# A two-layer encoder: the FFN in four rounds, its raw weights in activation buffers, its scale at the output sums

## The chip, the cores and the metric

The kernel runs on one core of a Trainium2 chip. The metric is the device time of one execution in microseconds, the median of several runs. The engines are TensorE (PE, matrix products into PSUM), VectorE (DVE), ScalarE (ACT), GpSimd (POOL), and SyncE (SP), whose queue starts most of the DMA transfers; GpSimd starts those that add to what lies at their target. Each engine takes its instructions in order.

## The reference

Two layers, each on x of 512 positions by 1024 channels, all in float32. The first part of a layer mixes attention, a convolution and a Fourier transform and ends in an output projection and a residual add. The change is in the second part, the FFN with D_FF = 2816:

```python
x = x + merged @ w_out[l]

h2 = rmsnorm(x, norm2_g[l])
f_gate, f_up = jnp.split(h2 @ w_ffn_in[l], 2, axis=-1)
x = x + (jax.nn.silu(f_gate) * f_up) @ w_ffn_out[l]
```

## The kernel before

Everything is held with channels on the 128 partitions and the 512 positions along a row; x is eight tiles of 128 x 512 (`x2[m]`). A float32 product is made of three matmuls at reduced precision: each operand is split into a high part (a copy to fp32r) and a low part (operand minus high part), and high x high, high x low and low x high are summed in PSUM. So every weight and every activation has two buffers.

Weights come in chunks of 128 x 1024 (512 KB), each loaded by SyncE into a `raw` buffer. `WB` gives the numbers of buffers for raw, high and low chunks: 3, 3 and 5. `chunk` (L192) prepares an ordinary chunk: a ScalarE copy gives the high part (L203), and a VectorE subtraction the low part (L205). In the FFN (`by_dma`, `low_by_dma` L275) the low part is made otherwise: ScalarE writes the negated raw weight, rounded, into the low buffer (L276), and a DMA started by GpSimd adds the weight from HBM to it (L277).

The FFN's hidden channels are 22 tiles of 128. One tile is a unit: a gate tile and an up tile, two sums over eight tiles of x. A unit is computed by the scheme of Strassen and Winograd with seven products instead of eight. `combine` (L296) makes the combinations of x once per layer (`us`, `ts`, in buffers of `at`, `X` and `B`); `pair_weights` (L232) makes those of the weights from two raw chunks (quarters a11, a12, a21, a22), with sums s1, s2, s4 on VectorE (L259, L263, L267), a difference written over a21 in the raw buffer (L260), high copies (L261, L266), and low parts (L262 for half of `l1`, by DMA for the other half and for `l2`). The sums' splits take buffers of `att` for the first four units of a layer, else of `A`. `pair_gemm` (L316) runs four products of 256 columns, copies and adds them to `p15` (L335, L336), then runs three more. Its two PSUM banks are of tag `s`, `att` or `main` in turn, by the unit's number modulo 3; `main` has three banks, the others two.

`unit` (L526) then scales gate and up by `rb2`, the inverse RMS of each position (L529 to L536), with Silu on ScalarE (L532), multiplies them (L537) and splits the result into buffers of `wth`, `wtl`, `qst`/`kst` or `att`. After eleven units, `gemm` makes eight output sums over these eleven tiles in `main` banks, and L556 adds each to `x2[m]`. The second half does the same with the other eleven; there x goes to HBM or, in layer 0, also to the next layer's first split (`next_x`, with L158 on VectorE and an addition L360 on GpSimd).

Before the FFN, the output projection runs over the split tiles `ms`, which lie in `cv` and `A`. For each of its sums the residual is loaded (L513), added (L517), scaled (L518) and combined.

The order of instructions on each engine is set by a planner that simulates the program; each piece has a due time (`self.at`). Weights of a unit are due `WLS` = 26000 ns before their use, ordinary chunks `WL` = 16000.

Of the kernel before, what the change touches and what calls it, by code (L numbers as in the profile page):

```python
# [9 lines left out]
F32 = mybir.dt.float32  # L10
# [3 lines left out]
ALU = mybir.AluOpType  # L14
AX = mybir.AxisListType

P = 128
# [43 lines left out]
WB = (3, 3, 5)  # L61
WLS = 26000
HALF = 108
PASS = 216
# [24 lines left out]
class Hybrid:  # L89
# [102 lines left out]
    def chunk(self, l, c, t):  # L192
# [8 lines left out]
        if self.by_dma:  # L201
            self.low_by_dma(lo, raw, self.a["w"][l, c])
        nc.scalar.copy(hi, raw)  # L203
        if not self.by_dma:
            nc.vector.tensor_tensor(out=lo, in0=raw, in1=hi.bitcast(F32), op=ALU.subtract)  # L205
# [26 lines left out]
    def pair_weights(self, early):  # L232
# [3 lines left out]
        raws = []  # L236
        for _ in range(2):
            raw = self.wp.tile([P, CHUNK * P], F32, tag="raw", name=self.nm("wr"), bufs=WB[0])
            c, k = divmod(self.wi, CHUNK)
            assert k == 0  # L240
            nc.sync.dma_start(raw, self.a["w"][self.l, c])
            self.wi += CHUNK
            raws.append(raw)
        r1, r2 = raws
        a21, a11 = r1[:, 0:T], r1[:, T : 2 * T]
        a22, a12 = r2[:, 0:T], r2[:, T : 2 * T]
        tags = ("qst", "kst", "ar") if early else ("cv", "cv", "cv")
        s1, s2, s4 = (self.slot(tag) for tag in tags)
        out = {}

# [4 lines left out]
        c = self.wi // CHUNK - 2  # L255
        self.low_by_dma(l1[:, T : 2 * T], a11, self.a["w"][self.l, c][:, T : 2 * T])
        self.low_by_dma(l2, r2, self.a["w"][self.l, c + 1])
        g = nc.vector.tensor_tensor
        g(out=s1, in0=a21, in1=a22, op=ALU.add)  # L259
        g(out=a21, in0=a11, in1=a21, op=ALU.subtract)  # L260
        nc.scalar.copy(h1, r1)  # L261
        g(out=l1[:, 0:T], in0=a21, in1=h1[:, 0:T].bitcast(F32), op=ALU.subtract)  # L262
        g(out=s2, in0=s1, in1=a11, op=ALU.subtract)  # L263
        for name, src in (("s1", s1), ("s2", s2)):
            out[name] = self.split_to(src, "att" if early else "A")
        nc.scalar.copy(h2, r2)  # L266
        g(out=s4, in0=a12, in1=s2, op=ALU.subtract)  # L267
        out["s4"] = self.split_to(s4, "att" if early else "A")
# [5 lines left out]

    def low_by_dma(self, lo, raw, src):  # L275
        self.nc.scalar.activation(lo, raw, AF.Copy, scale=-1.0)  # L276
        self.nc.gpsimd.dma_start(lo, src, accum_op=ALU.add)  # L277
# [193 lines left out]
    def main(self, l):  # L471
# [7 lines left out]
        self.by_dma = False  # L479
# [46 lines left out]
        def unit(j, b1, b2, qw):  # L526
# [9 lines left out]
            v(out=u, in0=u, in1=rb2, op=ALU.mult)  # L536
# [4 lines left out]
            if j < 7:  # L541
                return self.split_to(u, "qst", "kst")
            return self.split_to(u, "att")

        self.by_dma = True
        for half in range(2):
            act = []
            for j in range(NJ // 2):
                w = self.pair_weights(half == 0 and j < 4)
                got = self.pair_gemm(j, w, xc, half == 0 and j == 0)  # L550
                if half == 0 and j == 0:
                    rb2 = self.inv_rms(acc, D, "M", "rb")
                act.append(unit(j, *got))
            for m in range(KT):
                ps = self.gemm(act)
                nc.vector.tensor_tensor(out=x2[m], in0=ps, in1=x2[m], op=ALU.add)  # L556
                if half == 0:
                    continue
# [512 lines left out]
def _pack(inp, l):  # L1071
# [3 lines left out]
    def add(w):  # L1075
        seq.append(_tiles(w).reshape(-1, P, P))
# [35 lines left out]
    for half in range(2):  # L1112
        for j in range(half * NJ // 2, (half + 1) * NJ // 2):
            for k in range(2):
                for o in (FF, 0):
                    add(w1[k * D // 2 : (k + 1) * D // 2, o + j * P : o + (j + 1) * P])
        add(w2[half * FF // 2 : (half + 1) * FF // 2])
# [80 lines left out]
```

## Time and profile before

| what | value |
|---|---|
| median of 3 runs | 1646.55 us (1642.36 to 1651.85) |
| the profiled execution, its own time | 1652.3 us |
| its span in the profile | 1650.5 us |
| mean granted clock of TensorE | 0.99 |
| TensorE busy | 1601.2 us, 97% of the span |
| VectorE busy | 1247.5 us, 76% |
| ScalarE busy | 889.0 us, 54% |
| GpSimd busy | 229.3 us, 14% |
| moved by DMA | 236.47 MB |

In the profile a busy time is what an engine spent in instructions; for TensorE it includes pipelining, so a busy engine is not always one at its peak. A wait is put down to the instruction that ended it. The chain of waits follows the work that ended last back from the end, at each step to what released it. PEclk is the granted share of TensorE's full clock. In the views, a line number such as L262 is that of the kernel before, `wr` is a raw chunk, `wh`/`wl` are high and low parts of an ordinary chunk, `whi`/`wlo` of a unit's.

### The profile page before, as it was taken

How to read it: one execution, taken by the hardware profiler on the slowest of the kernel's cores; microseconds unless marked ns; L12 is line 12 of the kernel's file. 1: busy time of each engine (PE TensorE's matmuls, PEld its weight loads, DVE VectorE, ACT ScalarE, POOL GpSimd, SP SyncE). 2: the span in 40 equal slices, each digit the busy share in tenths (PEclk: the TensorE clock that was granted, in tenths of full speed). 3: DMA queues.
4: the chain of work that ended last, by engine and by line, in shares of the span. 5: the costliest groups of instructions: out<-in, count | busy, mean ns of one | idle time of the engine just before them, and what ended most of it. 6: DMA issues, size and time to landing. Idle time of an engine off the chain costs nothing.

```text
span 1650.5 us, 24460 instructions
## 1 busy us (share of the span) xinstructions
PE 1601.2 (97%) x9096; PEld 1397.1 (85%) x9096; DVE 1247.5 (76%) x2308; ACT 889.0 (54%) x1399; POOL 229.3 (14%) x217
## 2 busy tenths in 40 slices
PE   8999999999999999999999999998999899999999
PEld 6888888887889888999888888886878798889887
DVE  7899999897878833885269999997877887257840
ACT  6345555773566644666443455457535665545651
POOL 4000000113321111112200000000142111111110
PEclk8999999999999999999999999999999899999999
DMA  5545233322467797778743642332225667976784
GB/s 191 172 139 159 77 109 106 104 75 83 132 158 169 158 216 182 166 168 211 201 131 90 190 126 84 107 105 71 84 87 150 148 156 173 211 168 165 178 210 122
DMA packets 80471, 236.47 MB, mean 143 GB/s; under 512 B 11088, under 2 KB 11984, under 8 KB 80352
## 3 DMA queue, kind: packets, MB, share of 16 engines
q1 hardware_dynamic: 60912, 176.11, 33.4%
q0 software_dynamic: 19440, 58.81, 21.2%
q8 instruction: 71, 1.16, 0.3%
q14 instruction: 48, 0.39, 0.1%
HBM read 220.98 MB, written 13.89 MB: 142 GB/s over the span
## 4 chain that ended last, share of the span: by engine, by line
PE 72%; DMA 11%; DVE 11%; ACT 3%; issue 2%; SPq 0%; DVEq 0%; ACTq 0%
PE main L121 53%; DMA wr<-in_w 11%; PE s L121 4%; PE att L121 3%; PE oth L121 3%; PE att L288 3%; PE s L288 3%; PE att L131 2%; PE main L288 1%; DVE wr L260 1%; DVE cv L259 1%; DVE wlo L262 1%; DVE A L155 1%; DVE cv L263 1%; DVE cv L267 1%
## 5 line engine op out<-in xcount | busy, mean ns | idle before, releaser
L203 ACT CAST wh<-wr 128x1024 fp32r<-128x1024 f32 x180 | 188.5, 1049 | 210.7 <-PE main L121 103.4
L121 PE MATMUL main<-X,wh 128*128 128x512 f32 x864 | 278.3, 396 | 0.0
L205 DVE TENSOR_TENSOR wl<-wr,wh 128x1024 fp32r<-128x1024 f32 x136 | 178.6, 1313 | 28.9 <-ACT wh L203 28.0
L121 PEld LDWEIGHTS main<-X,wh 128*128 128x128 f32 x864 | 161.8, 189 | 32.6 <-issue 0.5
L997 DVE SCALAR_TENSOR_TENSOR cv<-cv,hcw,cv 128x497 f32<-128x497 f32 (+14 forms) x240 | 176.5, 735 | 1.3
L121 PE MATMUL main<-X,wl 128*128 128x512 f32 x432 | 170.3, 394 | 0.0
L276 ACT ACTIVATE wlo<-wr 128x512 fp32r<-128x512 f32 x88 | 74.0, 844 | 125.5 <-DMA wr<-in_w 120.4
L277 POOL DMA_DIRECT2D wlo<-in_w x88 | 76.5, 869 | 413.6 <-ACT wlo L276 286.5
L121 PE MATMUL main<-att,wh 128*128 128x512 f32 x384 | 119.6, 391 | 3.0 <-ACT att L154 3.0
L821 ACT ACTIVATE at<-s,mx 128x512 f32<-128x512 f32 x128 | 87.9, 688 | 62.2 <-DVE mx L819 58.3
L556 DVE TENSOR_TENSOR V<-main,V 128x512 f32<-128x512 f32 x32 | 22.1, 691 | 126.3 <-PE main L121 126.2
L121 PE MATMUL main<-A,wh 128*128 128x512 f32 x320 | 105.9, 391 | 0.0
L121 PE MATMUL main<-wh,X 128*128 128x512 f32 x288 | 96.5, 391 | 0.0
L121 PEld LDWEIGHTS main<-X,wl 128*128 128x128 f32 x432 | 81.7, 189 | 16.8 <-issue 0.2
L819 DVE TENSOR_REDUCE mx<-s 128x1 f32<-128x512 f32 x128 | 86.6, 681 | 5.1 <-PE s L121 4.6
L276 ACT ACTIVATE wl<-wr 128x1024 fp32r<-128x1024 f32 x44 | 46.6, 1059 | 80.5 <-DMA wr<-in_w 78.7
L121 PEld LDWEIGHTS main<-att,wh 128*128 128x128 f32 x384 | 71.7, 188 | 19.0 <-ACT att L154 3.5
L259 DVE TENSOR_TENSOR cv<-wr,wr 128x512 f32<-128x512 f32 x36 | 25.0, 693 | 82.3 <-DMA wr<-in_w 82.3
L121 PE MATMUL main<-cv,wh 128*128 128x512 f32 x240 | 78.1, 394 | 4.9 <-ACT cv L154 4.8
L121 PE MATMUL main<-act,wh 128*128 128x512 f32 x256 | 80.6, 394 | 0.2 <-ACT wh L203 0.2
L1028 POOL TENSOR_TENSOR cv<-cv,cv 128x512 f32<-128x512 f32 x6 | 9.0, 1492 | 510.1 <-DVE cv L997 449.8
L155 DVE TENSOR_TENSOR A<-cv,A 128x512 fp32r<-128x512 f32 x108 | 73.7, 684 | 3.6 <-ACT A L154 3.6
(329 smaller groups left out, 4326.9 us busy)
## 6 DMA issues: line engine op xcount, KB each, us to landing
wr<-in_w SPq DMA_DIRECT2D x268, 512.0 KB, 4.4
wlo<-in_w POOLq DMA_DIRECT2D x44, 512.0 KB, 5.6
wl<-in_w POOLq DMA_DIRECT2D x44, 512.0 KB, 7.3
wlo<-in_w POOLq DMA_DIRECT2D x44, 256.0 KB, 4.5
dqk<-at SPq DMA_DIRECT2D x32, 256.0 KB, 3.7
qst<-dqk SPq DMA_DIRECT2D x96, 64.0 KB, 1.9
kst<-dqk SPq DMA_DIRECT2D x96, 64.0 KB, 2.0
V<-in_xT SPq DMA_DIRECT2D x8, 256.0 KB, 7.5
```

What stands on the lines that cost most here:

```text
L121: return self.pin(self.nc.tensor.matmul(out, lhsT=lhsT, rhs=rhs, start=start, stop=stop))
L131: self.pin(self.nc.tensor.transpose(ps[:, s], src[:, s], self.ident))
L155: nc.vector.tensor_tensor(out=lo, in0=src, in1=hi.bitcast(F32), op=ALU.subtract)
L203: nc.scalar.copy(hi, raw)
L205: nc.vector.tensor_tensor(out=lo, in0=raw, in1=hi.bitcast(F32), op=ALU.subtract)
L259: g(out=s1, in0=a21, in1=a22, op=ALU.add)
L276: self.nc.scalar.activation(lo, raw, AF.Copy, scale=-1.0)
L277: self.nc.gpsimd.dma_start(lo, src, accum_op=ALU.add)
L288: self.nc.tensor.matmul(ps, lhsT=a[:, s], rhs=b, start=start and k == ks[0] and i == 0, stop=last and i == 2, skip_group_check=True,)
L819: nc.vector.tensor_reduce(out=mx, in_=ps, axis=AX.X, op=ALU.max, negate=True)
L821: nc.scalar.activation(e, ps, AF.Exp, bias=mx, accum_out=z1 if c else z0)
L997: ins = nc.vector.scalar_tensor_tensor(out=acc[:, a:b], in0=g[:, a + d : b + d], scalar=w[:, t : t + 1], in1=acc[:, a:b], op0=ALU.mult, op ...
```

## The change

The FFN runs in four rounds of 6, 6, 6 and 4 units instead of two of 11, each followed by eight output sums over its tiles. Raw weights of odd units go into four half buffers of 128 x 512, of `att` for unit 1 and of `cv` for the others; those of even units stay in `raw`. The first sums s1 and s2 lie in `ar` (unit 0), `att` (unit 1) or `cv`, s4 takes the place of s1, and the splits of the sums go to `A` for odd units and to `qst`/`kst` for even ones. High buffers become four and low ones four. The low part `l1` is now wholly a VectorE subtraction; `l2` is still made by the DMA. Chunks of the output weights are split like all others, by a VectorE subtraction. The product of the up branch with `rb2` is left out of `unit`; instead each output sum is multiplied by `rb2` into a buffer of `M` and then added to `x2[m]`. The weights are packed on the host in the new order.

```diff
--- before.py
+++ after.py
@@ -58,9 +58,10 @@
 PEORD = False
 CONV_LOW = -20000
 WL = 16000
-WB = (3, 3, 5)
+WB = (3, 4, 4)
 WLS = 26000
 HALF = 108
+ROUNDS = (6, 6, 6, 4)
 PASS = 216
 MAGIC = 0x5F3759DF
 
@@ -198,11 +199,8 @@
         nc.sync.dma_start(raw, self.a["w"][l, c])
         hi = self.wp.tile([P, CHUNK * P], F32R, tag="hi", name=self.nm("wh"), bufs=WB[1])
         lo = self.wp.tile([P, CHUNK * P], F32R, tag="lo", name=self.nm("wl"), bufs=WB[2])
-        if self.by_dma:
-            self.low_by_dma(lo, raw, self.a["w"][l, c])
         nc.scalar.copy(hi, raw)
-        if not self.by_dma:
-            nc.vector.tensor_tensor(out=lo, in0=raw, in1=hi.bitcast(F32), op=ALU.subtract)
+        nc.vector.tensor_tensor(out=lo, in0=raw, in1=hi.bitcast(F32), op=ALU.subtract)
         tc.cur_priority = keep
         return hi, lo
 
@@ -229,52 +227,65 @@
         self.at(self.t)
         return ps
 
-    def pair_weights(self, early):
+    def pair_raw(self, u):
+        nc = self.nc
+        c, k = divmod(self.wi, CHUNK)
+        assert k == 0
+        self.wi += 2 * CHUNK
+        out = []
+        for i in range(2):
+            src = self.a["w"][self.l, c + i]
+            if u % 2 == 0:
+                raw = self.wp.tile([P, CHUNK * P], F32, tag="raw", name=self.nm("wr"), bufs=WB[0])
+                nc.sync.dma_start(raw, src)
+                out.append((raw[:, 0:T], raw[:, T : 2 * T], raw))
+            else:
+                halves = []
+                for o in (0, T):
+                    half = self.slot("att" if u == 1 else "cv")
+                    nc.sync.dma_start(half, src[:, o : o + T])
+                    halves.append(half)
+                out.append((*halves, None))
+        return out, self.a["w"][self.l, c + 1]
+
+    def pair_weights(self, u):
         nc, tc = self.nc, self.tc
         keep = tc.cur_priority
         self.at(self.t - WLS)
-        raws = []
-        for _ in range(2):
-            raw = self.wp.tile([P, CHUNK * P], F32, tag="raw", name=self.nm("wr"), bufs=WB[0])
-            c, k = divmod(self.wi, CHUNK)
-            assert k == 0
-            nc.sync.dma_start(raw, self.a["w"][self.l, c])
-            self.wi += CHUNK
-            raws.append(raw)
-        r1, r2 = raws
-        a21, a11 = r1[:, 0:T], r1[:, T : 2 * T]
-        a22, a12 = r2[:, 0:T], r2[:, T : 2 * T]
-        tags = ("qst", "kst", "ar") if early else ("cv", "cv", "cv")
-        s1, s2, s4 = (self.slot(tag) for tag in tags)
+        ((a21, a11, r1), (a22, a12, r2)), src2 = self.pair_raw(u)
+        s1, s2 = (self.slot(("ar", "att")[u] if u < 2 else "cv") for _ in range(2))
+        tags = ("A", "A") if u % 2 else ("qst", "kst")
         out = {}
-
         h1, l1, h2, l2 = (
             self.wp.tile([P, CHUNK * P], F32R, tag=tag, name=self.nm("w" + tag), bufs=WB[i])
             for tag, i in (("hi", 1), ("lo", 2), ("hi", 1), ("lo", 2))
         )
-        c = self.wi // CHUNK - 2
-        self.low_by_dma(l1[:, T : 2 * T], a11, self.a["w"][self.l, c][:, T : 2 * T])
-        self.low_by_dma(l2, r2, self.a["w"][self.l, c + 1])
         g = nc.vector.tensor_tensor
+
+        def parts(raw, a, b):
+            return ((slice(0, T), a), (slice(T, 2 * T), b)) if raw is None else ((slice(0, 2 * T), raw),)
+
+        for o, x in parts(r2, a22, a12):
+            nc.scalar.activation(l2[:, o], x, AF.Copy, scale=-1.0)
+        nc.gpsimd.dma_start(l2, src2, accum_op=ALU.add)
         g(out=s1, in0=a21, in1=a22, op=ALU.add)
         g(out=a21, in0=a11, in1=a21, op=ALU.subtract)
-        nc.scalar.copy(h1, r1)
-        g(out=l1[:, 0:T], in0=a21, in1=h1[:, 0:T].bitcast(F32), op=ALU.subtract)
-        g(out=s2, in0=s1, in1=a11, op=ALU.subtract)
-        for name, src in (("s1", s1), ("s2", s2)):
-            out[name] = self.split_to(src, "att" if early else "A")
-        nc.scalar.copy(h2, r2)
-        g(out=s4, in0=a12, in1=s2, op=ALU.subtract)
-        out["s4"] = self.split_to(s4, "att" if early else "A")
+        g(out=s2, in0=a22, in1=a21, op=ALU.subtract)
+        for o, x in parts(r1, a21, a11):
+            nc.scalar.copy(h1[:, o], x)
+        out["s1"] = self.split_to(s1, *tags)
+        for o, x in parts(r1, a21, a11):
+            g(out=l1[:, o], in0=x, in1=h1[:, o].bitcast(F32), op=ALU.subtract)
+        out["s2"] = self.split_to(s2, *tags)
+        for o, x in parts(r2, a22, a12):
+            nc.scalar.copy(h2[:, o], x)
+        g(out=s1, in0=a12, in1=s2, op=ALU.subtract)
+        out["s4"] = self.split_to(s1, *tags)
         for names, hi, lo in ((("s3", "a11"), h1, l1), (("a22", "a12"), h2, l2)):
             for i, n in enumerate(names):
                 out[n] = (hi[:, i * T : (i + 1) * T], lo[:, i * T : (i + 1) * T])
         tc.cur_priority = keep
         return out
-
-    def low_by_dma(self, lo, raw, src):
-        self.nc.scalar.activation(lo, raw, AF.Copy, scale=-1.0)
-        self.nc.gpsimd.dma_start(lo, src, accum_op=ALU.add)
 
     def product(self, ps, w, xs, ks, start, stop):
         wh, wl = w
@@ -476,7 +487,6 @@
         hcw = sm(4 * CW, "hcw")
         nc.vector.tensor_scalar_mul(hcw, self.par(l, "cw"), 0.5)
         self.hb, self.hcw = hb, hcw
-        self.by_dma = False
         self.glu(l)
         if l == 0:
             self.tables()
@@ -533,28 +543,28 @@
             u = self.slot("M")
             v(out=u[:, 0:h], in0=b2[:, h:T], in1=qw[:, 0:h], op=ALU.add)
             v(out=u[:, h:T], in0=qw[:, 0:h], in1=qw[:, h:T], op=ALU.add)
-            v(out=u, in0=u, in1=rb2, op=ALU.mult)
             v(out=u, in0=u, in1=z, op=ALU.mult)
             if j < 4:
                 t = self.wtp.tile([P, 2, T], F32R, tag="wth" if j < 2 else "wtl", name=self.nm("act"))
                 return self.split(u, t[:, 0, :], t[:, 1, :])
-            if j < 7:
-                return self.split_to(u, "qst", "kst")
             return self.split_to(u, "att")
 
-        self.by_dma = True
-        for half in range(2):
+        done = 0
+        for rnd, nj in enumerate(ROUNDS):
             act = []
-            for j in range(NJ // 2):
-                w = self.pair_weights(half == 0 and j < 4)
-                got = self.pair_gemm(j, w, xc, half == 0 and j == 0)
-                if half == 0 and j == 0:
+            for j in range(nj):
+                w = self.pair_weights(done + j)
+                got = self.pair_gemm(done + j, w, xc, done + j == 0)
+                if done + j == 0:
                     rb2 = self.inv_rms(acc, D, "M", "rb")
                 act.append(unit(j, *got))
+            done += nj
             for m in range(KT):
                 ps = self.gemm(act)
-                nc.vector.tensor_tensor(out=x2[m], in0=ps, in1=x2[m], op=ALU.add)
-                if half == 0:
+                y = self.slot("M")
+                nc.vector.tensor_tensor(out=y, in0=ps, in1=rb2, op=ALU.mult)
+                nc.vector.tensor_tensor(out=x2[m], in0=y, in1=x2[m], op=ALU.add)
+                if done < NJ:
                     continue
                 if l == L - 1:
                     nc.sync.dma_start(self.out[m], x2[m])
...
```

## Rows read from the trace of the kernel before

**Rows 1.** windows, halves of both FFNs: stretch, us, engines busy (count), clock, DMA share
```profile
462.50:649.50 187.00, 178.47 (x1191) 163.71 (x1191) 119.67 (x216) 107.04 (x149) 32.86 (x37) 0.98 0.76 176
649.50:825.70 176.20, 172.94 (x1190) 160.95 (x1190) 106.18 (x192) 100.21 (x139) 33.30 (x36) 1.00 0.76 186
1278.50:1469.20 190.70, 179.12 (x1191) 165.05 (x1190) 119.32 (x216) 106.82 (x148) 32.63 (x37) 0.97 0.75 173
1469.20:1646.90 177.70, 173.22 (x1190) 160.65 (x1188) 98.12 (x183) 90.14 (x122) 25.17 (x29) 1.00 0.72 169
```

**Rows 2.** chain that ended last (start us, us, what): TensorE pieces without stall
```profile
71.53 2.04 PE main L121 x9
...
752.29 4.32 PE s L288 x36
```

**Rows 3.** TensorE waits, whole span (us in total, times, longest): L288
```profile
PE s L288 <- ACT whi L261: 8.5, 7, 3.6
...
PE s L288 <- DVE at L155: 4.8, 2, 2.4
...
PE main L288 <- ACT M L335: 2.8, 5, 1.1
PE main L288 <- ACT whi L261: 2.2, 2, 1.3
...
PE att L288 <- ACT whi L261: 1.9, 3, 1.0
...
PE s L288 <- ACT M L335: 0.8, 2, 0.4
```

**Rows 4.** chain within 670 to 715 us: one turn of loading
```profile
677.79 4.45 DMA wr<-in_w
...
687.14 0.70 DVE wlo L262
...
687.85 4.46 DMA wr<-in_w
```

**Rows 5.** waits of SyncE's DMA queue, whole span: unit weights
```profile
SPq L241 <- DVE wlo L262: 257.6, 34, 11.7
```

**Rows 6.** windows: just after the stall at 470.9 us in layer 0
```profile
470.90:477.10 6.20, 6.16 (x24) 5.13 (x25) 4.99 (x8) 2.89 (x5) 1.28 (x1) 0.52 0.70 165
```

**Rows 7.** timeline of SyncE's queue before the first FFN
```profile
456.12 9.43 SPq L241 DMA_DIRECT2D wr<-in_w  x2
465.60 0.42 SPq L513 DMA_DIRECT2D M<-in_xT  x1
```

**Rows 8.** timeline of ScalarE before the first FFN
```profile
460.05 0.63 ACT L276 ACTIVATE wlo<-wr 128x512 fp32r<-128x512 f32 x1 [5.42 <-DMA wr<-in_w]
```

**Rows 9.** VectorE groups, 462.5 to 1647 us: busy, mean ns, idle before
```profile
L205 DVE TENSOR_TENSOR wl<-wr,wh 128x1024 fp32r<-128x1024 f32 x68 | 89.0, 1309 | 19.6 <-ACT wh L203 19.4
...
L259 DVE TENSOR_TENSOR cv<-wr,wr 128x512 f32<-128x512 f32 x36 | 25.0, 693 | 82.3 <-DMA wr<-in_w 82.3
...
L556 DVE TENSOR_TENSOR V<-main,V 128x512 f32<-128x512 f32 x32 | 22.1, 691 | 126.3 <-PE main L121 126.2
```

**Rows 10.** windows: unit stretches of layer 0's second half
```profile
650.00:760.00 110.00, 106.74 (x881) 105.77 (x880) 87.08 (x164) 68.57 (x100) 17.33 (x20) 1.00 0.73 171
680.00:700.00 20.00, 20.00 (x167) 19.84 (x166) 18.00 (x35) 13.49 (x21) 3.45 (x4) 1.00 0.73 176
```

**Rows 11.** timeline of VectorE at the first border from units to sums
```profile
597.85 0.69 DVE L537 TENSOR_TENSOR M<-M,M 128x512 f32<-128x512 f32 x1 [5.13 <-ACT M L532]
```

**Rows 12.** timeline of GpSimd, end of layer 0
```profile
820.25 1.30 POOL L360 TENSOR_TENSOR M<-M,M 128x512 f32<-128x512 f32 x1 [6.28 <-ACT M L357]
```

**Rows 13.** timeline of VectorE, the same stretch
```profile
815.64 1.23 DVE L205 TENSOR_TENSOR wl<-wr,wh 128x1024 fp32r<-128x1024 f32 x1 [2.83 <-ACT wh L203]
...
821.12 1.51 DVE L205 TENSOR_TENSOR wl<-wr,wh 128x1024 fp32r<-128x1024 f32 x1 [0.75 <-ACT wh L203]
...
827.75 0.75 DVE L158 SCALAR_TENSOR_TENSOR B<-V,par,A 128x512 fp32r<-128x512 f32 x1
```

More of the change, by code (lines that the diff above doesn't have):

```diff
@@ L1111, in _pack @@
     w1, w2 = inp["w_ffn_in"][l], inp["w_ffn_out"][l]
-    for half in range(2):
-        for j in range(half * NJ // 2, (half + 1) * NJ // 2):
+    done = 0
+    for nj in ROUNDS:
+        for j in range(done, done + nj):
             for k in range(2):
@@ L1116, in _pack @@
                     add(w1[k * D // 2 : (k + 1) * D // 2, o + j * P : o + (j + 1) * P])
-        add(w2[half * FF // 2 : (half + 1) * FF // 2])
+        add(w2[done * P : (done + nj) * P])
+        done += nj
     s = np.concatenate(seq, 0)
```

## The prediction

> **What bounds the kernel now.** TensorE is the engine that the rest feeds, so I read first, by windows, the two FFN stages, the only place where the order of work changes: four halves of 187.0, 176.2, 190.7 and 177.7 us [rows 1], 731.6 in all. Then the chain that ended last, for what these halves would take with TensorE never waiting: nine 512-column matmuls follow each other in 2.04 us, 0.2267 each, and 36 of 256 columns in 4.32, 0.120 each [rows 2]. A unit (one `pair_gemm`) has 7 products of 12 narrow matmuls, 84 x 0.120 = 10.08 us; eleven make 110.9. The eight output sums of a half are 8 x 11 x 3 = 264 wide ones, 59.8 us. A half without a stall is 170.7. The four lose 16.3, 5.5, 20.0 and 7.0, together 48.8 us. This is all that the change can win: it leaves every matmul as it was.
>
> Third, TensorE's own waits on L288, for what these 48.8 are. For high halves of weights (`whi`) 8.5 + 2.2 + 1.9 = 12.6 us; for evictions of a unit (L335, L336) 8.0 in five groups, of which the first and the last on L335 are shown; for the activations' combinations (`at`) at the stage's start 4.8, with two smaller groups 6.0 [rows 3]. With 0.7 of others that is 27.3. The other 21.5 are refill of the pipeline behind each wait and stretches at the lower clock: the 6.2 us after the stall at 470.9 ran at a granted 0.52, near the lower of the two levels (1.2 of 2.4 GHz) [rows 6], and cost about 3.
>
> Last, the chain inside a unit stretch, which says why weights are late. A raw load takes 4.45 us, its `raw` buffer is free only after VectorE's L262, the next load starts behind that, and the turn from load to load is 687.85 - 677.79 = 10.06 us here [rows 4], as long as the unit itself, with nothing to spare. SyncE's queue says the same: its unit loads waited 34 times, 257.6 us in all, for L262 [rows 5]. The longest stall, 3.6 us, is a first product waiting for its high half [rows 3].
>
> **The change part by part.** *Raw weights in two pools.* Even units keep the three `raw` buffers, odd ones take four half buffers of `att` or `cv`; each pool then turns once in two units, 20.2 us of TensorE for a turn of about 10 to 11 [rows 4]. High buffers go from 3 to 4 and splits alternate between `A` and `qst`/`kst`, so a unit's weights no longer wait for its neighbour's products. I take all 12.6 us of `whi` waits as gone, with their part of the 21.5 of refill and clock, 21.5 x 12.6 / 27.3 = 9.9: 22.5 together. Next to come late are the evictions; their 8.0 + 6.3 I leave as they are (bounds: all won, or as much again lost: -14.3 to +14.3).
>
> *The stage's start.* At 456.12 SyncE took 9.43 us over two raw loads for lack of a buffer, and the residual's load L513 stood behind them until 465.60 [rows 7]; ScalarE stood 5.42 us before a negation whose raw had not landed [rows 8], with the scaling L518 that the combination needs queued behind it. So `at` came late. Unit 1's raw now goes to `att` buffers that are long free, and neither queue should stand so long. Against that, the splits of unit 1 go to `A`, which the output projection holds to its last matmul: ScalarE's copy waits there, and its other work (L518, L357) behind it. The start's price is 6.0 + 21.5 x 6.0 / 27.3 = 10.7; I take half, 5.4 (0 to 10.7).
>
> *VectorE's load.* Per layer: 22 output chunks split by a subtraction, x 1.309 = 28.8 us; `l1` whole instead of half, 22 x (1.309 - 0.693) = 13.6; 64 evictions of output sums where 16 were, so 48 more at 0.69 = 33.1; the 22 products with `rb2` gone, -15.2 (same size as L259) [rows 9]. That is +60.3 a layer, 120.6 for both. VectorE had 443.3 us in the four halves [rows 1]; 563.9 in stages of some 713 is a share of 0.79. It reached 0.79 over 110 us of units, and 0.90 over 20 us in which TensorE never stopped [rows 10], though it stood 82.3 us behind raw loads at L259 alone [rows 9]. It fits, and I cost it at nothing while it is covered by output sums, which had VectorE mostly idle and now come after 4 or 6 units instead of 11; what it costs without that cover is a rival below. Halves of the loads double the issues of odd units on SyncE; only loads queue there, with the residual and the results at the stage's ends. GpSimd keeps one accumulating DMA a unit of two, and none for output chunks; ScalarE loses the negations. I count no gain for these: neither is what TensorE waits for.
>
> *More borders.* Units give way to sums at eight borders instead of four. A sum can run only up to the last unit's tile before that unit is evicted. At the border at 591 us that tile's product with the gate (L537) came at 597.85, held 5.13 us by ScalarE's Silu [rows 11]; no stall followed, since three `main` banks with ten tiles each gave 3 x 10 x 3 x 0.2267 = 20 us of other work. In the new rounds of 6 a bank gives 3 x 5 x 0.2267 = 3.4 us, and units 5, 11 and 17, which end the first three, hold two of the three `main` banks themselves (`u % 3` is 2) until they are evicted; in the round of 4 three free banks give 6.1. So the cover is 3.4 to 10.2 us for a chain that took about 8 here, and ScalarE no longer has negations of chunks in its queue. Bounds per border 0 to about 5 (8 less 3.4), 0 to 40 in all; I take 1 each, 8, nearer to the lower end since 10.2 covers the row seen.
>
> *The ends.* After the last matmul there is one VectorE instruction more, 0.69 [rows 9]. At layer 0's end the last round has 12 matmuls per sum, 2.72 us, against VectorE's two evictions, half a chunk and the next layer's split, 0.69 + 0.69 + 0.65 + 0.75 [rows 9, 13] = 2.78. I take 1 us (0 to 11, below).
>
> Sum: -22.5 - 5.4 + 8 + 0.7 + 1 = -18.2 us. Against the profiled execution (span 1650.5, its own time 1652.3) that is 1634. It lay 5.75 above the median of the three runs; the same sum from the median 1646.55 gives 1628.
>
> **The rivals.** *All of it goes.* If the evictions follow the weights too, and borders are free, 46 of the 48.8 are won: 1601. For it: 20 us at 680 ran without a stall [rows 10]. Against: eviction waits have nothing to do with the ring.
>
> *The ring was mostly hidden.* Then only the 12.6 and some 3 of lower clock come back, and the eviction waits double by 8, since weights that are ready early stand in VectorE's queue ahead of evictions: -7, 1639. For it: TensorE waits only 12.6 us by name for weights [rows 3] while the loads wait 257.6 [rows 5]. It is also what comes if the extra buffers don't lengthen the turn.
>
> *VectorE becomes the bound (slower).* 563.9 us of work in order, with each wait of the queue's head paid by all behind it. At share s the two stages take 563.9 / s: as long as now at 0.771, and slower by over 0.5% (8.2 us) below 0.762; at 0.75 it is 751.9, +20, 1667. Place: the last two units of a round, where chunk subtractions come on top of the units' own 17 instructions, and sums whose banks wait for an eviction. For it: the 0.79 over 110 us is near [rows 10]. Against: that share was held down by the loads that the change frees.
>
> *The layer's end collides.* A subtraction of 1024 columns that began while GpSimd's 1.30 us addition ran [rows 12] took 1.51 us where another took 1.23 [rows 13]. In the last round there is one such addition per sum; if it shut VectorE out for all its length, each sum would need 2.78 + 1.30 = 4.08 against 2.72, 8 x 1.36 = 11 us late, 1638 in place of 1628. At the 0.28 seen it is 2, hidden by the three banks, and I hold to that. The Trainium skill, page "SBUF — State Buffer", section "SBUF: two separate sides", says that a VectorE instruction with two SBUF inputs and a GpSimd one that reads SBUF exclude each other for the whole instruction; by that rule the 11 us would be the upper end. The pair of rows agrees as far as the overlap goes.
>
> **How the numbers follow.** Forecast 0.53 (its own range 1614 to 1641: the start's 5.4 either way, the evictions' halves, a border of 0 to 2); all of it goes 0.10; layer's end 0.05; ring hidden 0.17; VectorE the bound 0.15. The range, 1606 to 1650, leaves out the slower case and half of the first rival. A measurement of this kernel tells about 0.5% from no change, so faster means below 1638.3: 0.53 + 0.10 + 0.05 less 0.05 for the forecast's upper edge, 0.63; within 0.5%: 0.17 + 0.05 = 0.22; slower 0.15.
>
> **What would show it.** Right: no `whi` waits to speak of in TensorE's list, SyncE's unit loads no longer waiting for the l1 subtraction, VectorE's share in the FFN near 0.79, stage lengths summing to about 713. Start right: L513 not behind a wait of raw loads, no clock of 0.5 after the first products. Borders wrong: idle before the first sums of a round longer than 1 us. Wrong altogether: TensorE waiting for VectorE at sums' banks or at p15, with VectorE busy over 0.85 ahead of it.

## The result, and the profile after

The changed kernel takes 1629.49 us (median of four runs, 1628.08 to 1630.56); the kernel before, timed again beside it, 1648.22 (four runs, 1642.36 to 1651.85). The ratio is 0.9889, with an interval of 0.9857 to 0.9921: 1.1% faster, 18.7 us between the medians. The profiled executions differ by 22.1 us of span, 1628.4 against 1650.5.

I read the new profile in the order of the old. First the windows of the FFN rounds (stretch, us, then busy time and instructions of PE, PEld, DVE, ACT and POOL, granted clock, DMA share, GB/s); they answer to [rows 1].

```profile
461.90:564.60 102.70, 97.57 (x654) 89.63 (x653) 79.25 (x135) 53.89 (x85) 13.11 (x9) 0.97 0.47 121
564.60:658.40 93.80, 93.80 (x651) 87.53 (x650) 72.55 (x123) 45.24 (x70) 5.21 (x6) 1.00 0.52 135
658.40:752.20 93.80, 93.80 (x650) 87.48 (x650) 71.80 (x122) 45.09 (x70) 5.22 (x6) 1.00 0.55 143
752.20:814.30 62.10, 62.10 (x432) 57.77 (x430) 45.10 (x71) 29.53 (x44) 5.51 (x5) 1.00 0.48 133
...
1270.00:1373.30 103.30, 97.82 (x653) 89.91 (x653) 79.84 (x136) 54.38 (x85) 13.50 (x9) 0.97 0.46 121
1373.30:1467.10 93.80, 93.80 (x650) 87.52 (x650) 72.81 (x123) 44.94 (x70) 5.22 (x6) 1.00 0.53 134
1467.10:1560.90 93.80, 93.80 (x650) 87.48 (x649) 72.17 (x122) 44.80 (x70) 5.21 (x6) 1.00 0.53 136
1560.90:1623.70 62.80, 62.76 (x433) 57.99 (x431) 40.72 (x70) 21.69 (x33) 1.73 (x2) 1.00 0.34 93
```

The eight stretches make 706.1 us where there were 731.6. By the pieces without a stall [rows 2], a round of six needs 6 x 10.08 + 8 x 6 x 3 x 0.2267 = 93.1 and the round of four 62.1, 682.8 in all. So 48.8 us above that floor have become 23.3. Six rounds lie within 0.7 us of it each, with TensorE busy throughout at the full clock. (In layer 0's last window the next layer's matmuls already run among the last sums, which end at 818.6; it holds as much work as a round of four, 432 matmuls, not that round alone.) The first round of each layer has the rest: 9.6 and 10.2 us. The DMA share, 0.72 to 0.76 in the halves before [rows 1], is now 0.34 to 0.55.

Next, TensorE's waits over the whole span (us in total, times, longest), which answer to [rows 3]:

```profile
PE oth L122 <- POOL M L371: 9.3, 2, 4.7
...
PE s L122 <- DVE B L159: 3.2, 3, 1.5
...
PE att L299 <- DVE wlo L278: 1.3, 2, 0.8
```

L299, the unit's matmul (L288 before), now waits 1.3 us for anything. The waits for high halves, 12.6 us, are gone; so are those for evictions, 8.0 us, and those for `at` at the start, 6.0 [rows 3]. The longest wait of the whole list is new: a GpSimd instruction, once per layer, 4.7 us. The timelines of GpSimd, of VectorE and of TensorE show it in layer 0 (start, us, engine, line, tile; in brackets the idle time before and what ended it):

```profile
469.48 6.13 POOL L371 TENSOR_TENSOR M<-M,M 128x512 f32<-128x512 f32 x1 [5.30 <-ACT M L368]
```

```profile
469.20 0.41 DVE L314 TENSOR_TENSOR ts<-us 128x256 f32<-128x256 f32 x1
469.53 0.41 DVE L315 TENSOR_TENSOR ts<-us,ts 128x256 f32<-128x256 f32 x1
469.87 0.68 DVE L272 TENSOR_TENSOR cv<-cv,cv 128x512 f32<-128x512 f32 x1
...
473.81 0.68 DVE L282 TENSOR_TENSOR cv<-cv,cv 128x512 f32<-128x512 f32 x1
477.78 0.69 DVE L379 TENSOR_SCALAR M<-oth 128x512 f32<-128x512 f32 x1 [3.28 <-PE oth L122]
```

```profile
470.63 0.40 PE L299 MATMUL att<-B,whi 128*128 128x256 f32 x2
475.67 2.07 PE L122 MATMUL oth<-M,ones 128*128 128x512 f32 x2 [4.64 <-POOL M L371]
```

L371 is the addition that gathers the squares for the norm; it is the last of seven, and TensorE's sum over partitions (`oth`) comes next in its order, ahead of the first unit's remaining products. The addition took 6.13 us in both layers; the 19 others from 432 us on in this trace took 1.28 to 1.99, and that of [rows 12] 1.30. VectorE meanwhile ran ten instructions without a gap until 474.49, and the addition ended 1.12 us later, at 475.61: by these times it stood until VectorE stopped, and then took nearly its usual time (tested below). TensorE was idle for 4.64 us (4.65 in layer 1), and the 5.40 us after it ran at a granted 0.57, as the 6.2 us after the old stall had run at 0.52 [rows 6]:

```profile
475.60:481.00 5.40, 5.33 (x22) 4.30 (x23) 1.72 (x3) 1.92 (x4) 0.01 (x1) 0.57 0.00 0
1284.00:1289.50 5.50, 5.41 (x20) 4.38 (x21) 1.62 (x3) 2.02 (x4) 0.04 (x1) 0.53 0.01 3
```

Last, what the page says of DMA issues (issue, count, KB each, median us from issue to landing), which bears on [rows 4]. First before, then after:

```profile
wr<-in_w SPq DMA_DIRECT2D x268, 512.0 KB, 4.4
wlo<-in_w POOLq DMA_DIRECT2D x44, 512.0 KB, 5.6
wl<-in_w POOLq DMA_DIRECT2D x44, 512.0 KB, 7.3
wlo<-in_w POOLq DMA_DIRECT2D x44, 256.0 KB, 4.5
```

```profile
wr<-in_w SPq DMA_DIRECT2D x224, 512.0 KB, 3.6
wlo<-in_w POOLq DMA_DIRECT2D x44, 512.0 KB, 5.6
cv<-in_w SPq DMA_DIRECT2D x80, 256.0 KB, 4.8
```

Of 132 accumulating transfers 44 are left, bytes moved fell from 236.47 to 201.85 MB, and a raw load lands in 3.6 us instead of 4.4 (the half loads of odd units, 256 KB each, in 4.8). In layer 1's FFN alone the raw loads' median was 5.7 before and is 3.7. This row turned out to matter more than the buffers that the change is named after.

### The profile page after: what moved, and what is told of

Same layout as the page of the kernel before. It is cut to its first block, busy times and chain, and to the rows that moved or that the text cites. A ratio compares the mean times of both kernels' runs of the same rounds, so it can differ in the third digit from the quotient of the medians.

```text
span 1628.4 us, 24344 instructions
## 1 busy us (share of the span) xinstructions
PE 1596.6 (98%) x9096; PEld 1394.5 (86%) x9096; DVE 1362.1 (84%) x2426; ACT 834.0 (51%) x1377; POOL 165.1 (10%) x129
## 2 busy tenths in 40 slices
DMA packets 74133, 201.85 MB, mean 124 GB/s; under 512 B 10384, under 2 KB 11280, under 8 KB 74016
## 4 chain that ended last, share of the span: by engine, by line
PE 88%; DVE 6%; ACT 2%; issue 2%; DMA 1%; POOL 1%; SPq 0%; DVEq 0%; ACTq 0%; POOLq 0%
PE main L122 50%; PE s L299 9%; PE main L299 9%; PE att L299 8%; PE s L122 3%; PE att L122 3%; PE oth L122 3%; PE att L132 2%; DVE wl L203 1%; POOL M L371 1%; DMA wr<-in_w 1%; DMA V<-in_xT 0%; DVE V L566 0%; PE att L723 0%; DVE V L527 0%
## 5 line engine op out<-in xcount | busy, mean ns | idle before, releaser
L203 DVE TENSOR_TENSOR wl<-wr,wh 128x1024 fp32r<-128x1024 f32 x180 | 231.0, 1284 | 31.9 <-ACT wh L202 30.8
L122 PE MATMUL main<-act,wh 128*128 128x512 f32 x512 | 162.0, 395 | 0.0
L122 PEld LDWEIGHTS main<-act,wh 128*128 128x128 f32 x512 | 95.2, 188 | 21.9 <-DVE M L565 1.2
L122 PE MATMUL main<-att,wh 128*128 128x512 f32 x320 | 100.1, 393 | 1.5 <-ACT att L155 1.5
L122 PE MATMUL main<-act,wl 128*128 128x512 f32 x256 | 101.1, 395 | 0.0
L270 POOL DMA_DIRECT2D wlo<-in_w x44 | 38.3, 870 | 571.3 <-ACT wlo L269 143.2
L565 DVE TENSOR_TENSOR M<-main,rb 128x512 f32<-128x512 f32 x64 | 43.3, 686 | 42.4 <-PE main L122 41.8
L122 PE MATMUL main<-A,wl 128*128 128x512 f32 x192 | 74.7, 392 | 0.0
L122 PEld LDWEIGHTS main<-A,wh 128*128 128x128 f32 x320 | 59.9, 188 | 12.5 <-issue 0.2
L122 PEld LDWEIGHTS main<-wh,X 128*128 128x128 f32 x288 | 54.0, 188 | 11.1
```

What stands on the lines that cost most here:

```text
L122: return self.pin(self.nc.tensor.matmul(out, lhsT=lhsT, rhs=rhs, start=start, stop=stop))
L270: nc.gpsimd.dma_start(l2, src2, accum_op=ALU.add)
L565: nc.vector.tensor_tensor(out=y, in0=ps, in1=rb2, op=ALU.mult)
```

## The experiments

My theory A was that of the prediction: the odd units' weights in buffers of their own broke the loop of load, subtraction and next load. Theory B: the extra high buffer did it. Theory C, formed on the row above: what counts is that 88 accumulating DMAs and their ScalarE negations are gone, which shortens the loads and ScalarE's queue. Theory S: the GpSimd stall is VectorE's unbroken run. The table gives medians, ratios to the kernel before in the same session (where its median was 1647.7 to 1651.8, so that across sessions the ratios compare better), and two lengths that I worked out from matmul starts in each trace: layer 0 from the first unit matmul to the first matmul into an `att` bank in layer 1, and layer 1 from its first unit matmul to the last matmul of the kernel. Differences are taken before rounding. What lies between them took 424.5 to 425.9 us, except 420.8 with `before, raw 4, low 5`, which also has one `at` buffer less and reaches layer 0's first unit 4.3 us later.

| kernel | us | ratio (interval) | layer 0 | layer 1 |
|---|---|---|---|---|
| before | 1648.22 | 1 | 391.0 | 368.0 |
| after | 1629.49 | 0.9889 (0.9857 to 0.9921) | 382.3 | 353.2 |
| after, one pool | 1621.92 | 0.9826 (0.9812 to 0.9841) | 378.7 | 348.5 |
| after, high 3 | 1629.74 | 0.9871 (0.9856 to 0.9886) | 380.5 | 355.1 |
| after, one pool, high 3 | 1616.02 | 0.9792 (0.9772 to 0.9811) | 375.8 | 346.8 |
| after, last square on VectorE | 1618.62 | 0.9809 (0.9786 to 0.9833) | 377.6 | 347.6 |
| after, extra VectorE work | 1630.23 | 0.9877 (0.9855 to 0.9898) | 382.8 | 353.7 |
| one pool, high 3, lows by DMA | 1647.51 | 1.0008 (0.9992 to 1.0024) | 390.2 | 362.6 |
| one pool, high 3, l1 by DMA | 1626.02 | 0.9861 (0.9823 to 0.9899) | 379.9 | 350.4 |
| one pool, high 3, rounds 8, 8, 6 | 1613.79 | 0.9801 (0.9780 to 0.9822) | 374.1 | 345.9 |
| one pool, high 3, splits in `A` | 1614.96 | 0.9809 (0.9789 to 0.9829) | 374.9 | 345.7 |
| before, raw 4, low 4 | 1653.65 | 1.0027 (1.0007 to 1.0048) | 396.4 | 364.4 |
| before, high 4, low 4 | 1633.14 | 0.9900 (0.9878 to 0.9921) | 383.0 | 356.4 |
| before, raw 4, low 5 | 1637.79 | 0.9919 (0.9897 to 0.9941) | 385.5 | 355.6 |

**Are the buffers the gain?** First the second pool is undone: all raw weights go through the three raw buffers.

```diff
-            if u % 2 == 0:
+            if True:
```

> The changed kernel with one edit: raw weights of all units go to the three raw buffers again, nothing to att or cv. Theory A (the ring of three raw buffers set the pace of the units): the units fall back from 10.1 to about 10.7 to 11 us, 44 units x 0.6 to 0.9 = 26 to 40 us less what the output sums between them let the loads catch up; I expect 1640 to 1652 us, with SyncE's unit loads waiting for VectorE's l1 and TensorE waiting for high halves. Rival B (it was the fourth high buffer and the alternating splits that freed the units): within 5 us of the changed kernel's 1629.

It came out 7.6 us faster than the changed kernel, not slower. Theory A falls with it. Then the fourth high buffer is undone in the changed kernel, and both together, which gives the three raw, three high and five low buffers of the kernel before:

```diff
-WB = (3, 4, 4)
+WB = (3, 3, 5)
```

> The changed kernel with 3, 3 and 5 buffers for raw, high and low chunks, as in the kernel before, instead of 3, 4 and 4. Theory A (raw ring): within 4 us of the changed kernel, 1626 to 1634. Rival B (the fourth high buffer): a unit's second high copy waits until the unit before has had its last products, TensorE waits for high halves at each unit, 10 us or more slower than the changed kernel, 1640 and up.

> The changed kernel with raw weights of all units in the three raw buffers, and 3, 3 and 5 buffers for raw, high and low chunks: rounds, split tags, splits on VectorE and the scale at the sums remain. Theory B (either more raw buffers or a fourth high one frees the units, and both are taken away here): the unit waits are back, 1636 to 1650 us. Rival (rounds, tags and VectorE splits did it, neither kind of buffer counts): within 5 us of 1622.

Without the fourth high buffer the time did not move, 1629.74, although this version has the long GpSimd addition in layer 1 only; what the missing stall gave must have been lost elsewhere, and where was not separated. With neither, the kernel is 13.5 us faster than the changed one. Theory B falls for the changed kernel too. In layer 1's FFN of this version TensorE was busy 345.59 of 346.80 us. So the gain is not in the buffers, and the two pools cost something.

**What do the two pools cost?** In the one-pool kernel the same addition of GpSimd took its usual time, and the two timelines (GpSimd, then VectorE) show what let it in:

```profile
469.32 1.29 POOL L371 TENSOR_TENSOR M<-M,M 128x512 f32<-128x512 f32 x1 [5.24 <-ACT M L368]
```

```profile
467.83 0.68 DVE L156 TENSOR_TENSOR A<-att,A 128x512 fp32r<-128x512 f32 x1
469.34 1.82 DVE L271 TENSOR_TENSOR cv<-wr,wr 128x512 f32<-128x512 f32 x1 [0.83 <-DMA wr<-in_w]
```

VectorE stood 0.83 us for a raw load that had no buffer earlier; GpSimd began in that gap, and now it is VectorE's instruction that took 1.82 us instead of 0.69. With two pools it works meanwhile on an odd unit's weights, whose `cv` buffers are filled (`cv<-cv,cv` above), VectorE never stands, and GpSimd does not get in. The changed kernel with three high buffers shows both cases in one execution, GpSimd and VectorE in layer 0 and then in layer 1:

```profile
467.84 1.28 POOL L371 TENSOR_TENSOR M<-M,M 128x512 f32<-128x512 f32 x1 [2.46 <-ACT M L368]
468.05 1.62 DVE L271 TENSOR_TENSOR cv<-cv,cv 128x512 f32<-128x512 f32 x1 [0.44 <-DMA cv<-in_w]
...
1274.19 7.32 POOL L371 TENSOR_TENSOR M<-M,M 128x512 f32<-128x512 f32 x1 [2.70 <-ACT M L368]
...
1279.71 0.69 DVE L282 TENSOR_TENSOR cv<-cv,cv 128x512 f32<-128x512 f32 x1
```

In layer 0 VectorE stood 0.44 us for a load and the addition took 1.28; in layer 1 VectorE ran on without a gap to 1280.40, and the addition took 7.32 and ended 1.11 us after that. To see whether this is the whole price, the last of the seven additions goes to VectorE, in the changed kernel with both pools:

```diff
-                acc = self.sq_add(xt, acc, "M")
+                if m == KT - 1:
+                    sq = self.sq_add(xt, None, "M")
+                    nc.vector.tensor_tensor(out=sq, in0=acc, in1=sq, op=ALU.add)
+                    acc = sq
+                else:
+                    acc = self.sq_add(xt, acc, "M")
```

> The changed kernel with the last of the seven additions of squares ahead of the FFN on VectorE instead of GpSimd. Theory S (GpSimd's addition, 6.13 us instead of 1.3, was shut out by VectorE's unbroken run of instructions, and TensorE then waited 4.64 us for it and ran on at the lower clock): the wait of the ones matmul goes in both layers, 6 to 8 us each less some delay of 0.7 in VectorE's queue, 1613 to 1622. Rival (the squares come late for another reason, such as the last residual or ScalarE): the wait stays under VectorE's name, 1626 to 1632.

The wait is gone from TensorE's list and the kernel takes 1618.62, 10.9 us less: the two stalls of 4.6 us and what followed them at the lower clock. Theory S holds. Without this stall two pools (1618.62) lie between one pool (1621.92) and one pool with three high buffers (1616.02), and the intervals of the ratios overlap with both.

**Had the loop of before any slack?** One more buffer in the kernel before, alone, of one kind or the other:

```diff
-WB = (3, 3, 5)
+WB = (4, 3, 4)
```

> The kernel before with 4, 3 and 4 buffers for raw, high and low chunks instead of 3, 3 and 5: only the load ring is longer. Theory A: a unit's two loads no longer wait for the unit before, the turn is paid once in two units, and 8 to 15 us of the 18.7 come, 1633 to 1640. Rival B (high buffers and splits are what holds the units): within 4 us of the kernel before, 1644 to 1652.

```diff
-WB = (3, 3, 5)
+WB = (3, 4, 4)
```

> The kernel before with 3, 4 and 4 buffers for raw, high and low chunks instead of 3, 3 and 5: only the high copies have one buffer more. Theory A: within 4 us of the kernel before, since the loads still wait for the same raw buffers, 1644 to 1652. Rival B: 8 us or more faster, 1640 and below.

A raw buffer in place of a low one gained nothing: TensorE now waited for low parts, 15.8 us on L288 over the whole span.

```profile
PE s L288 <- DMA wlo<-in_w: 9.8, 4, 3.8
...
PE att L288 <- DMA wlo<-in_w: 5.3, 4, 2.4
...
PE main L288 <- DMA wlo<-in_w: 0.7, 2, 0.5
```

A high buffer in place of a low one gained 19.6 us in the two stages of the profiled executions, 16.2 by the medians, the same kernel otherwise. To give the raw buffer its chance, the low ones stay at five, with an `at` buffer given up for room:

```diff
-WB = (3, 3, 5)
+WB = (4, 3, 5)
-        "X": 16, "A": 8, "B": 8, "V": 8, "att": 8, "cv": 8, "at": 5, ...
+        "X": 16, "A": 8, "B": 8, "V": 8, "att": 8, "cv": 8, "at": 4, ...
```

> The kernel before with 4, 3 and 5 buffers for raw, high and low chunks, so one raw buffer more and none taken from the low chunks; room is made by one `at` buffer less, which only the attention's exponentials feel. Read by the four FFN halves, 731.6 us before. Theory A (the raw ring alone set the pace, and the run with 4, 3 and 4 gained nothing only for its missing low buffer): the halves sum to 715 or less. Theory B (it was the number of high buffers): the halves stay at 726 to 736.

It gained 17.8 us in the stages, 14.0 by the medians; the profiled executions lie up to 4 us off the medians. So in the kernel before one buffer more, raw or high, is worth 14 to 20 us, somewhat less than the 22.5 that the prediction put on the waits for weights. The loop had no slack there, and it is these runs that show it. The two signs that I had read, a turn as long as a unit [rows 4] and loads that wait for the subtraction [rows 5], do not tell: one pool with three high buffers has both. SyncE's waits over the span of that version, and two low parts in layer 0's third round:

```profile
SPq L240 <- DVE wlo L278: 235.2, 36, 9.3
```

```profile
674.62 1.22 DVE L278 TENSOR_TENSOR wlo<-wr,whi 128x1024 fp32r<-128x1024 f32 x1
685.01 1.22 DVE L278 TENSOR_TENSOR wlo<-wr,whi 128x1024 fp32r<-128x1024 f32 x1
```

Its turn is 10.39 us here and its loads wait almost as long as before, yet TensorE was busy at the full clock for all of 655 to 715 us. What differs is whether the weights are ready when TensorE comes to them.

**If not the buffers, what loosened the loop in the changed kernel?** Starting from its fastest version so far, one pool and high 3, the low parts of the output weights and half of `l1` are made again as before: a negation by ScalarE and an accumulating DMA of GpSimd in place of the VectorE subtraction.

```diff
+        if self.by_dma:
+            nc.scalar.activation(lo, raw, AF.Copy, scale=-1.0)
+            nc.gpsimd.dma_start(lo, self.a["w"][l, c], accum_op=ALU.add)
...
+        nc.scalar.activation(l1[:, T : 2 * T], a11, AF.Copy, scale=-1.0)
+        nc.gpsimd.dma_start(l1[:, T : 2 * T], src1, accum_op=ALU.add)
...
-        for o, x in parts(r1, a21, a11):
-            g(out=l1[:, o], in0=x, in1=h1[:, o].bitcast(F32), op=ALU.subtract)
+        g(out=l1[:, 0:T], in0=a21, in1=h1[:, 0:T].bitcast(F32), op=ALU.subtract)
```

> The version with raw weights in three raw buffers and 3, 3 and 5 buffers (1616 us), with the low parts of output chunks and of the a11 halves made by ScalarE and a GpSimd DMA again, as in the kernel before; rounds, split tags and the scale at the sums remain. Theory C (fewer accumulating DMAs shorten the raw load from 4.8 to 3.7 us in unit stretches, and with it the turn of load and VectorE chain below a unit's 10.08 us): loads back to 4.5 us and more, the FFN of layer 1 (346.8 us) 10 to 20 us longer, 1632 to 1650. Rival D (rounds, tags or scale did it): within 6 us, 1612 to 1622.

All of it came back: 1647.51, the time of the kernel before, 31.5 us more. Theory C holds; the other direction, the kernel before with only these low parts moved to VectorE, was not run. The windows of layer 1's FFN, without and with these DMAs:

```profile
1262.50:1609.30 346.80, 345.59 (x2379) 321.12 (x2377) 268.10 (x438) 166.76 (x224) 20.67 (x23) 1.00 0.52 131
```

```profile
1277.80:1640.40 362.60, 351.63 (x2379) 323.11 (x2377) 232.69 (x417) 193.52 (x267) 56.95 (x65) 1.00 0.74 172
```

and the median to landing of the loads in the same two stretches:

```profile
wr<-in_w SPq DMA_DIRECT2D x61, 512.0 KB, 3.7
```

```profile
wr<-in_w SPq DMA_DIRECT2D x61, 512.0 KB, 5.6
```

VectorE does 35.4 us less work in the slower one; ScalarE does 26.8 more, the DMA share goes from 0.52 to 0.74, and a raw load takes 1.9 us longer. TensorE's waits of the kernel with the DMAs name ScalarE, for evictions and for high copies:

```profile
PE att L305 <- ACT M L352: 8.6, 11, 1.4
...
PE main L305 <- ACT whi L282: 3.8, 5, 1.2
```

These are the waits of [rows 3], evictions among them, in a kernel whose rounds, scale and tags are those of the changed one. Then `l1`'s half alone goes back to the DMA (the lines on `l1` in the diff above):

> The version with one pool and 3, 3 and 5 buffers (1616 us) with only the a11 half of l1 made by ScalarE and a GpSimd DMA again; output chunks stay split on VectorE. Theory E (the half lies in the loop of every unit: its transfer lengthens the raw loads, and ScalarE's negation stands in the queue ahead of the high copies): most of the 31.5 us that both kinds of DMA cost together come, 1634 to 1647, with raw loads of 4.3 us or more in unit stretches. Rival (the output chunks' DMAs did it, by holding up the first units of a round and taking transfers in the sums): within 6 us of 1616.

It costs 10.0 us of the 31.5 by the medians, 7.7 of 30.1 in the stages, with loads at 4.5 us in layer 1's FFN. The other 21.5 belong to the output weights' DMAs, or to both kinds together; that was not separated. Nor was the transfer from the negation that goes with it: the loads' 1.9 us speak for the first, the waits by name for the second, and neither proves its share.

**Do the other parts count?** From the same version, rounds of 8, 8 and 6, and then all splits but those of unit 0 in `A`, as they were before from the fifth unit on:

```diff
-ROUNDS = (6, 6, 6, 4)
+ROUNDS = (8, 8, 6)
```

> The same version with rounds of 8, 8 and 6 units instead of 6, 6, 6 and 4. Theory C: within 4 us, 1612 to 1620, by 16 evictions per layer less and two borders less rather faster. Rival D, its part on rounds (a short run of units can live on weights that were prepared during the sums): each round of 8 loses about 0.7 us in each unit beyond the sixth, 5 to 10 us slower.

```diff
-        tags = ("A", "A") if u % 2 else ("qst", "kst")
+        tags = ("A", "A") if u else ("qst", "kst")
```

> The same version with the splits of s1, s2 and s4 of all units but the first of a layer in `A`, eight buffers for six per unit, as in the kernel before, instead of alternating with `qst` and `kst`. Theory C: within 4 us, 1612 to 1620. Rival D, its part on tags (a unit's splits wait until its neighbour's products have read theirs, which keeps raw buffers held): 8 us or more slower, 1624 and up.

1613.79 and 1614.96 against 1616.02: the intervals overlap. In this version neither the number of rounds nor the alternating tags are worth anything that shows. The scale's move was not tried alone; in the kernel with lows by DMA it is there with rounds and tags, and all three together leave the time of before. Last, the slower rival: in the changed kernel two VectorE instructions more per unit that change nothing, 88 in all.

```diff
+            v(out=u, in0=u, in1=u, op=ALU.max)
+            v(out=u, in0=u, in1=u, op=ALU.max)
```

> The changed kernel with two more VectorE instructions of 128x512 in each unit (the maximum of u with itself, which changes nothing), 88 in all at 0.60 to 0.69 us, 53 to 60 us of work; VectorE's share in the FFN rises from 0.76 to 0.83 or 0.84. Theory (VectorE has slack that output sums give back): 0 to 5 us slower than the changed kernel. Rival (VectorE is at the edge of being the bound): 15 us or more slower, with TensorE waiting for it at p15 or at weights.

1630.23, as without them. The second round of layer 0, to be set beside 72.55 us of VectorE in the changed kernel:

```profile
564.60:658.40 93.80, 93.80 (x649) 87.34 (x649) 78.45 (x133) 45.22 (x69) 5.20 (x6) 1.00 0.53 134
```

At a share of 0.836 VectorE still holds nothing up.

## Why the prediction came out as it did

The time was right, 1628 against 1629.49, and so was the change of 18.2 against 18.7. The reason given for the largest term was not, and the agreement is in part luck: a stall that was not foreseen cost 10.9 us, while evictions and borders cost up to 22.3 less than forecast. Without that stall the kernel takes 1618.62, over 9 us below the forecast.

**Bound.** Right that the weights came late: relief by one buffer is worth 14 to 20 us, against the 22.5 put on it. The signs given for it [rows 4, 5] were not sufficient, as the fast version above has them too, and no run tests the sharing out of the refill in proportion to the named waits.

**Raw weights in two pools, -22.5.** The amount came, but not from there: with the second pool undone the kernel was 7.6 us faster. The step that failed stands two paragraphs further on: "GpSimd keeps one accumulating DMA a unit of two, and none for output chunks; ScalarE loses the negations. I count no gain for these: neither is what TensorE waits for." They were worth 31.5 us: with them back, the kernel takes the time of before. They lie in the loop, since a turn is a load plus the work up to the subtraction [rows 4]. I looked for them in TensorE's waits, where only the last link of a loop has a name. With them gone the old three raw and three high buffers are enough.

**Evictions, left at 8.0 + 6.3.** They went as well; that was the bounds' -14.3. The rival "all of it goes" said of them, against itself, that eviction waits had nothing to do with the ring. They had: with one high buffer more in the kernel before they fell from 8.0 to 3.2 us. Most of them name ScalarE, as the waits for high copies do [rows 3], and so they do again in the kernel with lows by DMA.

**The start, -5.4.** The steps named came true: the residual's loads (L523 now) no longer wait behind raw loads as at 456.12 [rows 7], and the waits for `at` (4.8 and one smaller group of 1.2, not two) went. This is SyncE's queue of the changed kernel:

```profile
453.11 1.93 SPq L240 DMA_DIRECT2D wr<-in_w  x2
455.09 3.25 SPq L523 DMA_DIRECT2D M<-in_xT  x2
458.40 1.84 SPq L246 DMA_DIRECT2D cv<-in_w  x4
```

But the early weights gave VectorE an unbroken run, and it shut out GpSimd's last addition: 10.9 us by the run without that stall. I had asked whom the early weights free, and not whom a busier VectorE keeps out. "No clock of 0.5 after the first products" was wrong with it.

**Borders, +8.** They cost nothing: rounds two and three are 0.7 us above their floor, borders included. The chain that made the eight us at the old border was ScalarE's [rows 11]: there the Silu stood behind the negation of an output chunk, which itself waited for its raw load. ScalarE at the old border, then at layer 0's first border now:

```profile
596.23 1.06 ACT L276 ACTIVATE wl<-wr 128x1024 fp32r<-128x1024 f32 x1 [3.14 <-DMA wr<-in_w]
597.20 0.62 ACT L532 ACTIVATE M<-M 128x512 f32<-128x512 f32 x1
```

```profile
627.34 0.63 ACT L542 ACTIVATE M<-M 128x512 f32<-128x512 f32 x1
```

From the first scaled half of the last unit to its product with the gate it took 8.4 us before (590.12 to 598.54), and 4.2 now (625.07 to 629.30). The prediction had said that ScalarE's queue would have no negations of chunks, and still took 8 us for the chain. The stages were forecast at about 713 us (711.7 by the terms) and took 706.1: the evictions' gain and the borders that cost nothing more than pay for the start.

**VectorE, 0.** Right. It was busy 534.25 us in the stages (268.70 and 265.55 in their two windows), not 563.9, a share of 0.757 of 706.1. The added work was forecast well, 120.6 us against 114.6 over the whole span; part of it fell outside the windows. A share of 0.836 in a round costs nothing, which ends the slower rival.

**Layer 0's end, +1.** About right; here VectorE and GpSimd meet in the other order. Timelines of VectorE and of TensorE:

```profile
820.28 1.80 DVE L566 TENSOR_TENSOR V<-M,V 128x512 f32<-128x512 f32 x1
...
822.91 0.69 DVE L566 TENSOR_TENSOR V<-M,V 128x512 f32<-128x512 f32 x1
823.52 2.35 DVE L203 TENSOR_TENSOR wl<-wr,wh 128x1024 fp32r<-128x1024 f32 x1
```

```profile
827.62 0.50 PE L122 MATMUL s<-B,wh 128*128 128x512 f32 x1 [1.00 <-DVE B L159]
```

An instruction that follows GpSimd's start is longer by 1.1 us, not by the 0.28 of [rows 13], so that rival's price, 1.30 for the addition's whole length, was nearer for a single instruction; three banks still hid all but about 1 us of it. The rule that the prediction took from the Trainium skill, page "SBUF — State Buffer", section "SBUF: two separate sides", that the pair of ports is held for the whole instruction by the one that starts first, agrees with this order, 1.80 against 0.69. At the start the order is the other, and 6.13 against 1.29 spans many VectorE instructions, which the rule for one instruction does not state. I had weighed this meeting of the two engines at the layer's end only, and it cost time at the start.

**The last eviction, +0.7.** There, 0.69 us of L566 after the last matmul.

## What to carry to other kernels

A turn as long as the consumer's step, or loads that wait for a buffer, do not tell whether a ring of buffers has slack; the consumer's waits, and a run with one buffer more, do. Then look for everything that lengthens the turn, other transfers and the queues of the engines in it included, and not only for a buffer to add: here taking out 88 accumulating transfers and their negations was worth 31.5 us against 14 to 20 for one buffer, and made the extra buffers needless. When a change lets an engine run without gaps, ask which small instruction of another engine used to slip into those gaps. The version to go on from is one pool and three high buffers, with `l1` and the output weights' low parts on VectorE, 1616.02, or 1613.79 in rounds of 8, 8 and 6, against 1629.49.

## What the runs showed of the hardware

A GpSimd addition of 128x512 that takes 1.29 us took 6.13 while VectorE ran ten instructions back to back on tiles in SBUF: it was kept out over many instructions, not one, though by the trace it had begun before nine of them. A gap of 0.44 us in VectorE's work was enough to let it in. The other way round, a VectorE instruction of 0.69 us took 1.80 to 1.82 after GpSimd's start. And with the 88 transfers that add into SBUF, and the negations before them, the plain loads beside them took a median of 5.6 us instead of 3.7 in layer 1's FFN.
